# Four modulation sixths summed on TensorE from raw weight tiles, token-major gate values, and raw tiles issued earlier, in a one-core decoder layer

## The chip, the cores and the metric

The kernel runs on one core of a Trainium2 chip. The metric is the device time of one launch in microseconds; the time before is the median of three runs.

## What is computed

One layer over 2048 tokens of width 1024, all in fp32. A conditioning vector gives six modulation vectors, `mod = silu(c) @ w_ada + b_ada` (1024 by 6144), in the order shift1, scale1, gate1, shift2, scale2, gate2. Then:

```
h    = rms_norm(x, g_mix) * (1 + scale1) + shift1
proj = h @ w_in                       # gMLP u | v (512 each), q, k, v
a    = u' * (tril(w_s) @ v' + b_s)    # u', v' = gelu(u), gelu(v); chunks of 128 tokens, 8 groups of 64
b    = sliding-window attention with sinks (8 q heads, 2 kv heads, window 128)
x    = x + gate1 * (concat(a, b) @ w_out)
h2   = rms_norm(x, g_ffn) * (1 + scale2) + shift2
x    = x + gate2 * (relu(h2 @ w_ff1)**2 @ w_ff2)
y    = rms_norm(x, g_final)
```

## The kernel before

Activations lie feature-major: tiles of 128 channels by 512 tokens (a slab; there are four). Each product is made in three matmuls (`mm3`, L326 to L328): operands are split into a high part on ScalarE (L69, L293) and a low part on VectorE (L70, L294), and high by high, high by low and low by high are summed in PSUM. The feed-forward layer works on a pair of slabs with a Strassen-like scheme of seven products: `ffn_c` makes the first half and writes its forms to DRAM (`ad`), `ffn_d` reads them back in 56 steps, each of two tiles `w2w` and `aw` (128x1024) that are split into `w2h`, `w2l`, `ah`, `al` and feed 24 matmuls of 512 columns.

The stages follow each other in the order of the code: slab 0's input projections, slabs 1 and 2 with attention 0 and 1 woven in (145 to 505 us), `ffn_c(0)` (505 to 820 us), `ffn_d(0)` with `beside` (slab 3, attention 2 and 3, output projections 2 and 3) woven into it (820 to 1452 us), `ffn_c(1)` (1452 to 1760 us) and `ffn_d(1)` to the end. The side work is written as generators that are advanced between matmul groups (`step`, `weave`). A scheduler then fixes the order of each engine's queue; every queue is executed in order. Nearly all transfers are issued on SP's queue: `get` issues a load, `put` appends a store that is issued one or two loads later.

Tiles come from pools with fixed numbers of slots, and a new tile waits until a slot is free: `wk` has 12 (weights, raw tiles, halves), `xl` has 4 (x tiles, w2 quarters), the PSUM bank `ov` has one.

`ada_rest(ci)` (L187 to L206) makes one sixth of the modulation in two halves. A half loads four `adar` tiles (128x2x512), and VectorE sums the eight raw tiles times a scalar into `acc` (L196, the first on ScalarE, L198); then four matmuls against a column of ones sum over the partitions. An fp32 matmul stands in the trace as two instructions, so these are 8. `in_vu` makes the gate: values are computed feature-major, transposed on TensorE (`turn`, L532), split and multiplied by the spatial weights (`gate`, L546 to L548). `out_proj` loads the residual tile `xt` after the group that it is added to (L719). `final_norm` stores `y` at L1059.

Of the kernel before, what the change touches and what calls it, by code (L numbers as in the profile page):

```python
# [11 lines left out]
F32 = mybir.dt.float32  # L12
F32R = mybir.dt.float32r
# [4 lines left out]
P = 128  # L18
D = 1024
KT = D // P  # L20
# [29 lines left out]
def hybrid_block(ctx, tc, x_l, c_l, pos, wada0, wada, vec, win, wsT, bs, sinks, wout, w1, w2, rope_c, y_l):  # L50
# [135 lines left out]

    def ada_rest(ci):  # L187
        for half in range(2):
            acc = t2("acc")
            for k in range(KT):  # L190
                if k % 2 == 0:
                    two = wk("adar", F32, [P, 2, T])
                    get(two, wada[ci - 2, half, k:k + 2].rearrange("k p t -> p k t"))
                raw, sc = two[:, k % 2], cact[:, k:k + 1]
                if k:
                    dve.scalar_tensor_tensor(out=acc, in0=raw, scalar=sc, in1=acc, op0=ALU.mult, op1=ALU.add)  # L196
                else:
                    act.activation(out=acc, in_=raw, func=AF.Copy, scale=sc)  # L198
                if k % 4 == 3:
                    yield  # L200
            mp = ps.tile([P, 4], F32, name="modp", tag="ov", bufs=1)
            for j in range(4):
                pe.matmul(out=mp[:, j:j + 1], lhsT=acc[:, j * P:(j + 1) * P], rhs=ones[:, 0:1], start=True, stop=True)
            o = ci * KT + 4 * half
            dve.tensor_tensor(out=mod[:, o:o + 4], in0=mp, in1=vecs[:, o:o + 4], op=ALU.add)
            yield  # L206
# [307 lines left out]
    def in_vu(s, h, st, u0=None):  # L514
        vts, us = {}, {}
        sgu = list(wsp)
        if s > 0:
            ts = [m2("wsp", F32R, [P, 4, P]) for _ in range(4)]
            for t, d in zip(ts, wspd):
                get(t.bitcast(F32).rearrange("p g c -> p (g c)"), d, d)  # L520
            sgu = [ts[0:2], ts[2:4]]

        def gelu(bank, name):
            t = t2(name)
            act.activation(out=t, in_=bank, func=AF.Gelu_apprx_tanh)
            return t

        def turn(p):
            vf = vts.pop(p)
            vp = ps.tile([P, NB, P], F32, name="vq", tag="pt", bufs=2)  # L530
            for b in range(NB):
                pe.transpose(out=vp[:, b], in_=vf[:, b * P:(b + 1) * P], identity=ident)  # L532
            vh, vl = m2("vt", F32R, [P, NB, P]), m2("vt", F32R, [P, NB, P])
            act.activation(out=vh, in_=vp, func=AF.Copy)
            dve.tensor_tensor(out=vl, in0=vp, in1=vh, op=ALU.subtract)
            vts[p] = vh, vl

        def gate(p):
            u, (vh, vl) = us.pop(p), vts.pop(p)
            sv = t2("sv")  # L540
            w_h, w_l = (t[:, 2 * (p % 2):2 * (p % 2) + 2] for t in sgu[p // 2])
            for half in range(2):
                so = ps.tile([P, 2, 2, P], F32, name="so", tag="sc", bufs=2)
                for i in range(2):
                    b = 2 * half + i
                    pe.matmul(out=so[:, i], lhsT=vh[:, b], rhs=w_h, start=True, stop=False)  # L546
                    pe.matmul(out=so[:, i], lhsT=vl[:, b], rhs=w_h, start=False, stop=False)
                    pe.matmul(out=so[:, i], lhsT=vh[:, b], rhs=w_l, start=False, stop=True)  # L548
                for hh in range(2):
                    r0, r1 = hh * HD, (hh + 1) * HD  # L550
                    dve.tensor_tensor(out=sv[r0:r1, half * 2 * P:(half + 1) * 2 * P].rearrange("p (c t) -> p c t", c=2),
                                      in0=so[r0:r1, :, hh, :],
                                      in1=bsb[r0:r1, p, :].unsqueeze(1).broadcast_to([HD, 2, P]), op=ALU.add)
            dve.tensor_tensor(out=sv, in0=sv, in1=u, op=ALU.mult)
            put(mixd[s][p], mixd[s][p], sv)

        todo = []

        def behind():
            while todo:  # L560
                f, p = todo.pop(0)
                f(p)

        for pp in range(2):
            two = w_take(("i", 4 * pp), ("i", 4 * pp + 1)), w_take(("i", 4 * pp + 1), ("i", 4 * pp + 2 + (pp == 0 and u0 is not None)))
            for p in (2 * pp, 2 * pp + 1):
                o = bank()
                for k in range(KT):
                    c = (k % 4) * 2 * P + (p % 2) * P
                    mm3(o, *two[k // 4].cut(c, c + P), h[k], k == 0, k == KT - 1)  # L570
                vts[p] = gelu(o, "vf")
                behind()
                todo.append((turn, p))
                yield
            for p in (2 * pp, 2 * pp + 1):
                if p == 0 and u0 is not None:
                    us[p] = u0
                else:
                    us[p] = gelu(group(h, ("i", 4 * pp + 2 + p % 2), ("i", min(4 * pp + 3 + p % 2, 7))), "u")
                    behind()  # L580
                    yield
                todo.append((gate, p))
        behind()
        yield


# [127 lines left out]

    def out_proj(s, mix):
        stat = Stat()
        for d in range(KT):
            o = group(mix, ("o", d), ("o", min(d + 1, KT - 1)))
            xt = x_tile(s, d)  # L719
            x2 = t2("x2")  # L720
            dve.scalar_tensor_tensor(out=x2, in0=o, scalar=mod[:, 2 * KT + d:2 * KT + d + 1], in1=xt,  # L721
                                     op0=ALU.mult, op1=ALU.add)
            stat.add(x2)
            put(x2d[s][d], x2d[s][d], x2)
            yield
# [121 lines left out]
    def ffn_c(p, forms):  # L847
# [42 lines left out]
        for j in range(16):  # L890
# [20 lines left out]
            if j > 0:  # L911
                product(j, 2, x, False)
                b11 = relu2(p1, x)
            prep(j + 1, 1)
            yield
            q = bank("mm")
            product(j, 7, q, True)
# [12 lines left out]
            dve.tensor_tensor(out=u, in0=q, in1=u, op=ALU.add)  # L930
            b21 = relu2(u)
            prep(j + 1, 3)
            load(j + 2)
            for i, f in token_forms(b11, b12, b21, b22).items():
                if i not in (1, 3):
                    nc.sync.dma_start(out=ad[p, i, c][:, e], in_=f)
# [6 lines left out]
    def ffn_d(p, last):  # L943
# [29 lines left out]
            dve.tensor_tensor(out=dst, in0=src, in1=dst, op=ALU.add)  # L973

        order = (1, 6, 5, 3, 7, 4, 2)
        halves = {}

        def prep(n):
            if n >= 56 or n in halves:
                return  # L980
            i, c = order[n // 8], n % 8
            wraw, araw = wk("w2w", F32), wk("aw", F32, [P, 2, T])
# [6 lines left out]
            get(araw, ad[p, i, c])  # L989
            halves[n] = (halve(wraw, wk("w2h"), wk("w2l")),  # L990
                         halve(araw, wk("ah", F32R, [P, 2, T]), wk("al", F32R, [P, 2, T])))

        for m, i in enumerate(order):
            if i in (1, 3, 7, 4):
# [43 lines left out]
            if i == 7:  # L1038
                norm = final_norm(2 * p + 1, xs, 1, stats[1])
            if i == 2:  # L1040
                last.append(final_norm(2 * p, xs, 0, stats[0]))
            yield

    def final_norm(s, xs, t, stat):
        stat.finish("sc")
        yield
        stat.diag()
        yield
        rbc = stat.cast(t2("rbc"), "sc")
        yield  # L1050
        for d in range(KT):
            x = xs[d // 4, t, d % 4]
            if x is None:
                x = sb.tile([P, T], F32, name="xt", tag="xl", bufs=NXL)
                get(x, x3d[d // 4, t, d % 4], x3d[d // 4, t, d % 4])
            y = t2("y")
            dve.scalar_tensor_tensor(out=y, in0=x, scalar=gfin[:, d:d + 1], in1=rbc,
                                     op0=ALU.mult, op1=ALU.mult)
            nc.sync.dma_start(out=y_l[s, d], in_=y)  # L1059
            if d % 2:  # L1060
                yield

# [182 lines left out]
    def beside():  # L1245
        rb3, h3, m2_, m3_ = [], [], [], []
        st2, st3 = sts[2], sts[3]
        rope_load(3)
        yield from zipped(chain(qkv_back(2, st2), then_halo(2, late(attention, 2, st2)), late(qkv_back, 3, st3)),
                          chain(x_stats(3, rb3), h_build(3, rb3, h3), in_qkv(3, h3, st3), in_vu(3, h3, st3)))  # L1250
        yield from zipped(attention(3, st3), chain(blank(28), mix_build(2, m2_), out_proj(2, m2_)))
        yield from mix_build(3, m3_)
        yield from until(h2, "even")
        yield from out_proj(3, m3_)

    def blank(n):
        for _ in range(n):
# [82 lines left out]
```

## Time and profile before

| | us |
|---|---|
| median of three runs | 2080.46 (2079.78 to 2086.93) |
| profiled execution, its time | 2078.88 |
| profiled execution, span | 2077.1 |
| TensorE busy | 1921.9 |
| VectorE busy | 1419.1 |
| ScalarE busy | 911.2 |

The span runs from the first instruction to the last. TensorE's matmuls are pipelined, so its busy time isn't its time at its peak; the start-to-start distance of neighbouring matmuls is the measure used below. The granted clock is 1.00 at TensorE's upper level and 0.50 at the lower; over the span it is 0.968.

### The profile page before, as it was taken

The page shows a single profiled execution, that of the slowest core. Times are in us where ns is not written, and L with a number is a line of the kernel's source. Part 1 is how long each engine was busy: PE and PEld are TensorE (multiplying, and loading weights), DVE is VectorE, ACT ScalarE, POOL GpSimd, SP SyncE. Part 2 cuts the span into 40 slices and gives each one's busy share as a digit, 9 for nine tenths or more (in the row PEclk, how much of TensorE's full clock was granted, in tenths as well). Part 3 has the DMA queues.
Part 4 walks back from the last instruction along what each step waited for, and adds up shares of the span by engine and source line. Part 5 has one row for each costly group of instructions (what it writes and reads, how often), then busy time and mean ns, then how long its engine had stood idle before and what let it go on. Part 6 is the DMA issues. An engine that isn't in the chain of part 4 may idle for free.

```text
span 2077.1 us, 25303 instructions
## 1 busy us (share of the span) xinstructions
PE 1921.9 (93%) x8532; PEld 1565.3 (75%) x8532; DVE 1419.1 (68%) x2400; ACT 911.2 (44%) x1563; POOL 173.9 (8%) x234
## 2 busy tenths in 40 slices
PE   5998898888999899889978998988999999999997
PEld 4787676777877688768866786866888888888875
DVE  8677789659677766783577855596766665545675
ACT  3535554244444444543344534354444444434442
POOL 4402213100000000010011210000000000000000
PEclk9999898999999999999988999999999999999998
DMA  9995497892577857787666789684544446555663
GB/s 319 352 348 200 130 329 260 307 388 84 197 269 247 276 177 267 262 310 249 205 203 227 283 295 343 223 293 143 183 149 156 157 152 210 193 200 210 235 218 128
DMA packets 236210, 486.72 MB, mean 234 GB/s; under 512 B 23808, under 2 KB 81280, under 8 KB 236080
## 3 DMA queue, kind: packets, MB, share of 16 engines
q1 hardware_dynamic: 234960, 484.38, 67.1%
q8 instruction: 67, 1.10, 0.2%
q0 software_dynamic: 1120, 0.72, 0.1%
q14 instruction: 63, 0.52, 0.1%
HBM read 349.55 MB, written 135.46 MB: 233 GB/s over the span
## 4 chain that ended last, share of the span: by engine, by line
PE 48%; DMA 8%; DVE 5%; ACT 2%; issue 1%; SPq 1%; POOL 0%; POOLq 0%; DVEq 0%; ACTq 0%
PE mm L327 16%; PE mm L328 15%; PE mm L326 15%; DMA w2w<-in_w_dram 2%; DMA aw<-ad 1%; DVE al L70 1%; DMA w2w<-w2d 1%; DMA a<-in_w_dram 1%; DVE w2l L70 1%; DMA w2d<-a 1%; ACT w2h L69 1%; PE sc L625 1%; DMA xt<-x2d 1%; DMA s<-w2d 1%; SPq L93 1%
## 5 line engine op out<-in xcount | busy, mean ns | idle before, releaser
L327 PE MATMUL mm<-al,w2h 128*128 128x512 f32 x896 | 357.4, 399 | 10.0 <-DVE al L70 9.7
L328 PE MATMUL mm<-ah,w2l 128*128 128x512 f32 x896 | 354.2, 396 | 0.0
L326 PE MATMUL mm<-ah,w2h 128*128 128x512 f32 x896 | 316.7, 400 | 13.7 <-ACT ah L69 13.1
L70 DVE TENSOR_TENSOR w2l<-w2w,w2h 128x1024 fp32r<-128x1024 f32 x112 | 137.3, 1226 | 181.7 <-ACT w2h L69 173.0
L69 ACT ACTIVATE w2h<-w2w 128x1024 fp32r<-128x1024 f32 x112 | 118.6, 1059 | 296.6 <-DMA w2w<-w2d 156.3
L327 PEld LDWEIGHTS mm<-al,w2h 128*128 128x128 f32 x896 | 171.6, 192 | 55.4 <-DVE al L70 20.5
L326 PEld LDWEIGHTS mm<-ah,w2h 128*128 128x128 f32 x896 | 171.0, 192 | 53.4 <-ACT ah L69 17.7
L326 PE MATMUL mm<-h,whi 128*128 128x512 f32 x448 | 181.3, 414 | 22.8 <-ACT h L264 12.8
L328 PEld LDWEIGHTS mm<-ah,w2l 128*128 128x128 f32 x896 | 171.3, 191 | 34.9
L327 PE MATMUL mm<-h,whi 128*128 128x512 f32 x448 | 180.6, 404 | 2.9 <-DVE h L265 2.7
L328 PE MATMUL mm<-h,wlo 128*128 128x512 f32 x448 | 179.8, 402 | 1.0 <-DVE wlo L294 0.9
L70 DVE TENSOR_TENSOR al<-aw,ah 128x1024 fp32r<-128x1024 f32 x112 | 137.3, 1226 | 34.6 <-ACT ah L69 21.0
L69 ACT ACTIVATE ah<-aw 128x1024 fp32r<-128x1024 f32 x112 | 118.4, 1058 | 60.0 <-DVE w2l L70 21.9
L234 POOL TENSOR_TENSOR rs<-ms,mhalf 128x4 f32<-128x4 f32 x12 | 16.6, 1386 | 1313.9 <-DVE ms L232 1313.8
L326 PEld LDWEIGHTS mm<-h,whi 128*128 128x128 f32 x448 | 87.9, 197 | 43.9 <-ACT h L264 14.4
L326 PE MATMUL mm<-mix,whi 128*128 128x512 f32 x256 | 100.9, 399 | 15.4 <-DVE x L721 9.5
L326 PE MATMUL mm<-hw,wah 128*128 128x512 f32 x256 | 100.8, 394 | 10.5 <-ACT p L895 9.3
L327 PEld LDWEIGHTS mm<-h,whi 128*128 128x128 f32 x448 | 87.2, 195 | 22.4 <-DVE h L265 5.1
L328 PE MATMUL mm<-mix,wlo 128*128 128x512 f32 x256 | 100.9, 394 | 1.4 <-DMA wlo<-ko2l 0.5
L328 PEld LDWEIGHTS mm<-h,wlo 128*128 128x128 f32 x448 | 87.1, 194 | 19.4 <-DVE wlo L294 1.3
L326 PE MATMUL mm<-hw,wdh 128*128 128x512 f32 x256 | 100.0, 391 | 1.1 <-DVE w L918 1.1
L326 PE MATMUL mm<-hw,wbh 128*128 128x512 f32 x256 | 100.2, 391 | 0.6 <-DVE w L908 0.6
(253 smaller groups left out, 4051.3 us busy)
## 6 DMA issues: line engine op xcount, KB each, us to landing
aw<-ad SPq DMA_DIRECT2D x112, 512.0 KB, 5.1
r<-in_w_dram SPq DMA_DIRECT2D x64, 512.0 KB, 5.0
w2w<-w2d SPq DMA_DIRECT2D x64, 512.0 KB, 3.7
a<-in_w_dram SPq DMA_DIRECT2D x96, 256.0 KB, 4.0
ad<-wt SPq DMA_DIRECT2D x96, 256.0 KB, 2.2
w2w<-in_w_dram SPq DMA_DIRECT2D x96, 256.0 KB, 3.9
xt<-in_x_dram SPq DMA_DIRECT2D x80, 256.0 KB, 6.1
adar<-in_wada_dram SPq DMA_DIRECT2D x32, 512.0 KB, 6.1
```

Of the source, the lines that this page charges most:

```text
L69: act.activation(out=hi, in_=t, func=AF.Copy)
L70: dve.tensor_tensor(out=lo, in0=t, in1=hi, op=ALU.subtract)
L93: ins = nc.sync.dma_start(out=out, in_=in_)
L234: self.pow = pool.tensor_tensor(out=rs[:, :nb], in0=ms[:, :nb], in1=mhalf[:, :nb], op=ALU.pow)
L326: pe.matmul(out=out, lhsT=wh, rhs=h[0], start=first, stop=False, **kw)
L327: pe.matmul(out=out, lhsT=wh, rhs=h[1], start=False, stop=False, **kw)
L328: last_mm[0] = pe.matmul(out=out, lhsT=wl, rhs=h[0], start=False, stop=last, **kw)
L625: pe.matmul(out=sc[:, i, o:o + (P if b == 0 else 2 * P)], lhsT=qst[:, j], rhs=key, start=hl == 0, stop=hl == 1)
```

## The change

- `ada_rest`: the eight raw tiles are no longer summed on VectorE and ScalarE. All four `adar` tiles of a half stay in their `wk` slots until 32 fp32 matmuls (four column blocks by eight tiles, the raw tile as the weights, one column of `cact` as the moving operand) sum them in PSUM.
- `in_vu`: values are computed token-major: the activation is the stationary operand, 256 columns of the weight the moving one. The transposes are gone. The next weight is no longer taken a group ahead for the u groups.
- `out_proj`: the residual tile is loaded one step ahead.
- `ffn_c`: the raw tiles of step j+2 are loaded after the fourth of seven products in place of the last.
- `ffn_d`: `load` is split from `prep`, and the raw tiles of the step after are loaded as soon as a step's are split.
- `final_norm`: `y` is stored through `put`, but for the last slab pair's first half.
- `beside`: `out_proj(3)` is interleaved with the first half of `h2_build(1)`, which stood ahead of it.

```
 def ada_rest(ci):
     for half in range(2):
-        acc = t2("acc")
-        for k in range(KT):
-            if k % 2 == 0:
-                two = wk("adar", F32, [P, 2, T])
-                get(two, wada[ci - 2, half, k:k + 2]...)
-            raw, sc = two[:, k % 2], cact[:, k:k + 1]
-            if k:
-                dve.scalar_tensor_tensor(out=acc, in0=raw, scalar=sc, in1=acc, op0=ALU.mult, op1=ALU.add)
-            else:
-                act.activation(out=acc, in_=raw, func=AF.Copy, scale=sc)
-            if k % 4 == 3:
+        twos = []
+        for k in range(0, KT, 2):
+            two = wk("adar", F32, [P, 2, T])
+            get(two, wada[ci - 2, half, k:k + 2]...)
+            twos.append(two)
+            if k % 4 == 2:
                 yield
         mp = ps.tile([P, 4], F32, name="modp", tag="ov", bufs=1)
         for j in range(4):
-            pe.matmul(out=mp[:, j:j + 1], lhsT=acc[:, j * P:(j + 1) * P], rhs=ones[:, 0:1], ...)
+            for k in range(KT):
+                pe.matmul(out=mp[:, j:j + 1], lhsT=twos[k // 2][:, k % 2, j * P:(j + 1) * P],
+                          rhs=cact[:, k:k + 1], start=k == 0, stop=k == KT - 1)
...
 # in_vu
-    def turn(p): ...                  # 4 transposes, then vh, vl from PSUM
+    def tokens(pp):
+        w = w_take(("i", 4 * pp), ("i", 4 * pp + 1)), w_take(("i", 4 * pp + 1))
+        for half in range(2):
+            o = bank()
+            ov = o.rearrange("p (b c) -> p b c", b=2)
+            for b in range(2):
+                cols = slice((2 * half + b) * P, (2 * half + b + 1) * P)
+                for k in range(KT):
+                    hi, lo = w[k // 4].cut((k % 4) * 2 * P, (k % 4 + 1) * 2 * P)
+                    pe.matmul(out=ov[:, b], lhsT=h[k][0][:, cols], rhs=hi, ...)
+                    pe.matmul(out=ov[:, b], lhsT=h[k][1][:, cols], rhs=hi, ...)
+                    last_mm[0] = pe.matmul(out=ov[:, b], lhsT=h[k][0][:, cols], rhs=lo, ...)
+            vf = gelu(o, "vf")
+            vh, vl = m2("vt"), m2("vt")   # split from vf
...
 # out_proj
+    xts = [x_tile(s, 0)]
     for d in range(KT):
+        if d + 1 < KT:
+            xts.append(x_tile(s, d + 1))
         o = group(mix, ("o", d), ("o", min(d + 1, KT - 1)))
-        xt = x_tile(s, d)
+        xt = xts[d]
...
 # ffn_c
         prep(j + 1, 1)
+        load(j + 2)
         yield
...
         prep(j + 1, 3)
-        load(j + 2)
...
 # ffn_d
     def prep(n):
         if n >= 56 or n in halves:
             return
+        load(n)
+        wraw, araw = raws[n]
         halves[n] = (halve(wraw, wk("w2h"), wk("w2l")),
                      halve(araw, wk("ah", F32R, [P, 2, T]), wk("al", F32R, [P, 2, T])))
+        load(n + 1)
...
 # final_norm
-            nc.sync.dma_start(out=y_l[s, d], in_=y)
+            if late:
+                put(y_l, y_l[s, d], y)
+            else:
+                nc.sync.dma_start(out=y_l[s, d], in_=y)
...
 # beside
-        yield from until(h2, "even")
-        yield from out_proj(3, m3_)
+        yield from zipped(out_proj(3, m3_), until(h2, "even"))
```

## Rows read from the trace of the kernel before

**Rows 1.** The page's head: the span, then busy time by engine.

```profile
span 2077.1 us, 25303 instructions
...
PE 1921.9 (93%) x8532; PEld 1565.3 (75%) x8532; DVE 1419.1 (68%) x2400; ACT 911.2 (44%) x1563; POOL 173.9 (8%) x234
```

**Rows 2.** Stages: length, busy time and instructions by engine, granted clock, DMA share, GB/s.

```profile
145.00:400.00 255.00, 220.80 (x1039) 177.51 (x1038) 210.00 (x537) 123.00 (x330) 58.47 (x79) 0.94 0.70 242
...
505.00:820.00 315.00, 302.05 (x1306) 246.26 (x1307) 219.87 (x311) 138.52 (x200) 0.00 (x0) 0.98 0.67 229
820.00:1250.00 430.00, 396.66 (x1772) 320.51 (x1771) 289.61 (x598) 190.43 (x408) 55.51 (x65) 0.95 0.74 254
...
1350.00:1452.00 102.00, 88.97 (x355) 68.10 (x354) 78.71 (x106) 48.79 (x65) 0.00 (x0) 0.95 0.67 222
1452.00:1960.00 508.00, 508.00 (x2247) 420.73 (x2246) 311.18 (x381) 229.63 (x293) 2.45 (x1) 1.00 0.53 183
```

**Rows 3.** TensorE in order of time, 170 us: start, length, line, operation.

```profile
170.34 0.95 PE L203 MATMUL modp<-ones,acc 128*128 128x1 f32 x8
171.15 0.49 PE L327 MATMUL mm<-h,whi 128*128 128x512 f32 x1
```

**Rows 4.** The tile adar: instructions, nanoseconds least, median, most.

```profile
L196 DVE SCALAR_TENSOR_TENSOR acc<-adar,cact,acc x56: 711/744/754, 143.9 to 681.0; 128x512 f32<-128x512 f32 x56
...
L198 ACT ACTIVATE acc<-adar,cact x8: 707/722/724, 141.7 to 640.4; 128x512 f32<-128x512 f32 x8
```

**Rows 5.** TensorE in order of time, 28 us.

```profile
28.36 1.70 PE L178 MATMUL modp<-ones,acc 128*128 128x1 f32 x8
29.92 0.77 PE L328 MATMUL mm<-h,wlo 128*128 128x512 f32 x1
```

**Rows 6.** TensorE in order of time, 52 to 58 us.

```profile
52.45 1.05 PE L178 MATMUL modp<-ones,acc 128*128 128x1 f32 x8 [0.63 <-DVE mod L182]
54.28 3.36 PE L326 MATMUL mm<-h,whi 128*128 128x512 f32 x7 [0.77 <-ACT h L264]
```

**Rows 7.** Half microseconds there, columns as in rows 2.

```profile
53.50:54.00 0.50, 0.01 (x1) 0.00 (x0) 0.50 (x1) 0.50 (x1) 0.41 (x2) 1.00 1.05 426
...
54.50:55.00 0.50, 0.50 (x2) 0.41 (x3) 0.50 (x1) 0.50 (x1) 0.42 (x2) 0.50 1.00 410
```

**Rows 8.** TensorE, 221 us: first and last of twelve matmuls of 256 columns.

```profile
221.29 0.28 PE L546 MATMUL so<-wsp,vt 128*128 128x256 f32 x1
...
222.61 0.28 PE L548 MATMUL so<-wsp,vt 128*128 128x256 f32 x1
```

**Rows 9.** TensorE, 94 us: four transposes and the matmul behind them.

```profile
94.74 0.60 PE L532 MATMUL vq<-ident,vf 128*128 128x128 f32 x4
95.09 0.48 PE L326 MATMUL mm<-h,whi 128*128 128x512 f32 x1
```

**Rows 10.** What TensorE waited for, 820 to 1250 us: total, times, longest.

```profile
PE sc L625 <- DVE pr L628: 4.6, 3, 3.5
PE tpp L658 <- DVE pr L649: 4.4, 3, 2.2
```

**Rows 11.** What ScalarE waited for, 820 to 1250 us.

```profile
ACT w2h L69 <- DMA w2w<-w2d: 68.6, 18, 9.5
```

**Rows 12.** What TensorE waited for, 1250 to 1452 us.

```profile
PE mm L326 <- ACT ah L69: 10.3, 6, 3.4
PE mm L326 <- DVE x L721: 9.5, 1, 9.5
```

**Rows 13.** The chain that ended last: start, length, what.

```profile
1402.21 3.69 DMA w2w<-in_w_dram
...
1408.94 4.30 DMA w2w<-in_w_dram
```

**Rows 14.** What SP's queue waited for, 1960 us to the end.

```profile
SPq L1059 <- DVE y L1057: 28.4, 13, 23.2
```

**Rows 15.** What TensorE waited for, 505 to 820 us.

```profile
PE mm L326 <- ACT p L895: 9.3, 5, 3.9
```

More of the change, by code (lines that the diff above doesn't have):

```diff
@@ L188, in ada_rest @@
         for half in range(2):
-            acc = t2("acc")
-            for k in range(KT):
-                if k % 2 == 0:
-                    two = wk("adar", F32, [P, 2, T])
-                    get(two, wada[ci - 2, half, k:k + 2].rearrange("k p t -> p k t"))
-                raw, sc = two[:, k % 2], cact[:, k:k + 1]
-                if k:
-                    dve.scalar_tensor_tensor(out=acc, in0=raw, scalar=sc, in1=acc, op0=ALU.mult, op1=ALU.add)
-                else:
-                    act.activation(out=acc, in_=raw, func=AF.Copy, scale=sc)
-                if k % 4 == 3:
+            twos = []
+            for k in range(0, KT, 2):
+                two = wk("adar", F32, [P, 2, T])
+                get(two, wada[ci - 2, half, k:k + 2].rearrange("k p t -> p k t"))
+                twos.append(two)
+                if k % 4 == 2:
                     yield
@@ L202, in ada_rest @@
             for j in range(4):
-                pe.matmul(out=mp[:, j:j + 1], lhsT=acc[:, j * P:(j + 1) * P], rhs=ones[:, 0:1], start=True, stop=True)
+                for k in range(KT):
+                    pe.matmul(out=mp[:, j:j + 1], lhsT=twos[k // 2][:, k % 2, j * P:(j + 1) * P],
+                              rhs=cact[:, k:k + 1], start=k == 0, stop=k == KT - 1)
             o = ci * KT + 4 * half
@@ L526, in gelu @@
             return t
[L528 to L536, printed above, removed]
+        def tokens(pp):
[7 more added lines that the diff above has]
+                        hi, lo = w[k // 4].cut((k % 4) * 2 * P, (k % 4 + 1) * 2 * P)
+                        pe.matmul(out=ov[:, b], lhsT=h[k][0][:, cols], rhs=hi, start=k == 0, stop=False)
+                        pe.matmul(out=ov[:, b], lhsT=h[k][1][:, cols], rhs=hi, start=False, stop=False)
+                        last_mm[0] = pe.matmul(out=ov[:, b], lhsT=h[k][0][:, cols], rhs=lo, start=False,
+                                               stop=k == KT - 1)
+                vf = gelu(o, "vf")
+                vh, vl = m2("vt"), m2("vt")
+                act.activation(out=vh, in_=vf, func=AF.Copy)
+                dve.tensor_tensor(out=vl, in0=vf, in1=vh, op=ALU.subtract)
+                vts[pp, half] = tuple(t.rearrange("p (b c) -> p b c", b=2) for t in (vh, vl))
+                yield
@@ L538, in gate @@
         def gate(p):
-            u, (vh, vl) = us.pop(p), vts.pop(p)
+            u = us.pop(p)
             sv = t2("sv")
+            cols = slice((p % 2) * P, (p % 2 + 1) * P)
             w_h, w_l = (t[:, 2 * (p % 2):2 * (p % 2) + 2] for t in sgu[p // 2])
             for half in range(2):
+                vh, vl = vts[p // 2, half]
                 so = ps.tile([P, 2, 2, P], F32, name="so", tag="sc", bufs=2)
                 for i in range(2):
[L545 to L548, printed above, removed]
+                    pe.matmul(out=so[:, i], lhsT=vh[:, i, cols], rhs=w_h, start=True, stop=False)
+                    pe.matmul(out=so[:, i], lhsT=vl[:, i, cols], rhs=w_h, start=False, stop=False)
+                    pe.matmul(out=so[:, i], lhsT=vh[:, i, cols], rhs=w_l, start=False, stop=True)
@@ L555, in gate @@
             put(mixd[s][p], mixd[s][p], sv)
[L557 to L562, printed above, removed]
-        for pp in range(2):
[L565 to L573, printed above, removed]
+        for pp in range(2):
+            for _ in tokens(pp):
+                if pp and 1 in us:
+                    gate(1)
                 yield
             for p in (2 * pp, 2 * pp + 1):
[L576 to L580, printed above, removed]
+                us[p] = u0 if p == 0 and u0 is not None else gelu(group(h, ("i", 4 * (p // 2) + 2 + p % 2)), "u")
+                if p % 2:
+                    gate(p - 1)
+                if p > 0 or u0 is None:
                     yield
-                todo.append((gate, p))
-        behind()
+        gate(3)
         yield
@@ L975, in ffn_d, with load @@
         order = (1, 6, 5, 3, 7, 4, 2)
-        halves = {}
-        def prep(n):
-            if n >= 56 or n in halves:
+        raws, halves = {}, {}
+        def load(n):
+            if n >= 56 or n in raws:
                 return
             i, c = order[n // 8], n % 8
-            wraw, araw = wk("w2w", F32), wk("aw", F32, [P, 2, T])
+            wraw, araw = raws[n] = wk("w2w", F32), wk("aw", F32, [P, 2, T])
             if i in W2SRC:
@@ L989, in prep @@
             get(araw, ad[p, i, c])
+        def prep(n):
+            if n >= 56 or n in halves:
+                return
+            load(n)
+            wraw, araw = raws[n]
             halves[n] = (halve(wraw, wk("w2h"), wk("w2l")),
                          halve(araw, wk("ah", F32R, [P, 2, T]), wk("al", F32R, [P, 2, T])))
+            load(n + 1)
         for m, i in enumerate(order):
@@ L1040, in ffn_d, with final_norm @@
             if i == 2:
-                last.append(final_norm(2 * p, xs, 0, stats[0]))
+                last.append(final_norm(2 * p, xs, 0, stats[0], p == 0))
             yield
-    def final_norm(s, xs, t, stat):
+    def final_norm(s, xs, t, stat, late=True):
         stat.finish("sc")
```

## The prediction

> **What bounds the kernel now.** I read the page's head first: TensorE is busy 1921.9 of 2077.1 us and VectorE, the next, 1419.1 [rows 1]. So time on TensorE's queue costs the kernel directly, unless it falls into a hole. The view of stages shows where the holes are [rows 2]. In 1452 to 1960 us TensorE never pauses: 2247 matmuls in 508 us, one per 0.226 us at a granted clock of 1.00. That is the rate at which a stream of 512 columns runs, and nothing can be won there. Elsewhere two things are lost, idle time and time at the lower clock, which I count as one minus the granted clock times the stage. From 145 to 400 us that is 34.2 us idle and some 15 us of clock, together about 50 of 255; from 820 to 1250 us it is 33.3 and 21.5, about 55 of 430; from 1350 to 1452 us 13 and 5; from 505 to 820 us 13 and 6. The waits of TensorE in these stages say what the holes are made of. From 820 to 1250 us they are mostly attention steps held by VectorE (4.6 us before the scores, 4.4 before the transposes) [rows 10], while ScalarE, whose queue those steps share, stands 68.6 us before `w2h` until a `w2w` load lands [rows 11].
>
> **The modulation sums: TensorE's new work.** Before, a half of a sixth costs TensorE 8 instructions. They take from 170.34 to 171.15 us, when the next matmul starts: 0.81 us, 0.101 each [rows 3]. Afterwards it is 32 matmuls of two instructions, 64. What a one-column instruction costs doesn't depend on which column it is, since what it waits for is its own weight load; so a train takes 64 x 0.101 = 6.5 us, 5.66 more than before, and the eight halves 45.3 us.
>
> The trace has no train of 64. Two short ones show what happens to the clock. At 28 us, at the lower level, 8 take 29.92 - 28.36 = 1.56 us, 0.195 each [rows 5]. At 52 us TensorE idles 0.63 us, runs a train of 8, and idles 0.77 us; when matmuls begin at 54.28 us the granted clock, 1.00 at 53.5, is 0.50 [rows 6, 7], and 7 matmuls take 3.36 us where 1.58 would do, so 1.8 us are lost. [...] I therefore expect a train of 6.5 us to lose the clock about halfway: 32 x (0.195 - 0.101) = 3.0 us for its second half, and some 1.7 us for the matmuls behind it. Eight times 4.7 is 37.6 us. The bounds are no fall (0) and the lower level for a whole train and 1.8 us behind it, 64 x 0.094 + 1.8 = 7.8, eight times 62.
>
> The Trainium skill (TensorE: Matmul & The Clock Gate, Part 1) says that the gate follows how busy the array has recently been, and that the throttled state is the default, released by activity. Whether one column per weight load is activity, that part doesn't say. If it is, the trains cost 45.3 us; if it isn't, some 83 us.
>
> **What hides it.** VectorE loses 56 sums of 744 ns, 41.7 us, and ScalarE 8 of 722 ns, 5.8 us [rows 4]. Six of the eight halves lie between 145 and 400 us, where VectorE is busy 210 of 255 us and TensorE loses about 50. A train ahead of a wait shortens that wait, and 31 us less on VectorE shorten others. I let this take back 28 us, somewhat over half of the stage's loss; the bounds are 0 and 50. The last two halves stand in `ffn_c(0)`, where VectorE has room and nothing is hidden. Modulation in all: 45.3 + 37.6 - 28 = +55 us.
>
> **Token-major values.** Per slab 96 matmuls of 512 columns become 192 of 256. Twelve of these run from 221.29 to 222.61 us, 11 distances of 0.120 [rows 8]; 192 x 0.120 - 96 x 0.226 = +1.3 us, +5.4 for four slabs. Gone are 16 groups of four transposes, each 0.35 us to the next matmul, which is 0.09 us longer than the usual 0.39: 0.44 x 16 = -7.0 us [rows 9]. Splits and gelus keep their count. Sum -2 us. The u weights are no longer taken a group ahead. SP can issue them early all the same while `wk` has slots; only slab 0 also has to split them, and a split of some 2.3 us exposed at three groups would be +7, the upper bound.
>
> **The residual tile ahead, and `out_proj(3)` beside `h2`.** TensorE stands 9.5 us before an output projection whose residual add had no x tile [rows 12], and the clock falls behind it, which by the price above is 1.7 us. Both edits aim at this place: -11 us, between 0 and that.
>
> **Raw tiles earlier.** In `ffn_d` a load moves ahead by one step, so ScalarE should find its tile and let the attention steps behind it through. Of the 55 us lost from 820 to 1250 us I take two fifths, -22; the bounds are 0 and -55. From 1350 to 1452 us I take nothing. The loads of neighbouring steps come 6.7 us apart there [rows 13], not the 24 x 0.226 = 5.4 us of their matmuls: the `x3` tiles hold two of the twelve `wk` slots, two sets of halves hold eight, and so the raw tiles of the next step need the two slots that those of this step leave when they are split. Issuing them sooner doesn't free a slot. In `ffn_c` ScalarE's late tiles cost TensorE 9.3 us through `p1` [rows 15]. The earlier load helps these, but the four `adar` tiles now stay in `wk` until their matmuls, two steps later, in the same stage: I net it at -1 us, between -9 and +10.
>
> **The late store of y.** At the end SP stands 28.4 us before stores of `y` with weight loads behind them [rows 14]. Stored through `put`, they no longer hold the loads: -3 us (0 to -6, as TensorE idles little there).
>
> **Sum.** 55 - 2 - 11 - 22 - 1 - 3 = +16 us. The profiled execution took 2078.9 us, so 2094.9; it lies 1.6 us below the median of the runs shown, within their spread. I forecast 2095 us.
>
> **Rivals.** *The trains are nearly free.* If the array counts them as work, or other matmuls are ordered between their instructions, the clock holds and the 37.6 us vanish. Then 45.3 - 28 - 39 = -22 us: 2057. For it speaks VectorE's 82% in the stage of six halves; against it the fall behind a short train [rows 6, 7]. It ends on the faster side and decides from the point where a train costs less than about 8.5 us, since then the sum crosses zero.
>
> *The slots run out.* In `ffn_d` raw tiles held a step longer bring one step's use to ten of twelve `wk` slots, and each side weight with its successor wants four. Then the side weights come late in place of the raw tiles; the 22 us are not won, and a late weight behind perhaps a dozen side groups at 1 us each adds 12: 2095 + 34 = 2129. That this limit binds already, with two slots less, is in [rows 13]; against it, a stretch of `beside` uses few weights.
>
> *The edits do little.* TensorE's holes take the trains, and the loads move while their waits go elsewhere: 2079 give or take 10.
>
> **How the numbers follow.** About 10 us, 0.5%, is what a measurement of this kernel can tell from no change. The forecast has 0.42 and runs from 2080 to 2115 (0.12 of it within 0.5%, 0.30 above). The free trains have 0.30, from 2035 to 2072 (0.28 below, 0.02 within). The slots have 0.18, 2115 to 2145, all above. The last has 0.10 (0.06 within, 0.04 below). Faster 0.32, same 0.20, slower 0.48. The range that leaves out 2 in 10, the far ends of both outer cases, is 2045 to 2132; the forecast's own is 2080 to 2115.
>
> **What the changed profile would show.** The trains: `modp` at L199 or so with 512 instructions, 0.10 us apart, with a granted clock of 0.50 in their second half and behind them; at 0.10 throughout and 1.00 behind them the first rival holds. VectorE's busy time lower by about 42 us. No `vq`. From 145 to 400 us TensorE's idle time well under 34 us, though the stage is longer. From 820 to 1250 us ScalarE's 68.6 us before `w2h` at less than half; if they stay, or TensorE waits for `whi` and `wlo` loads, the slots are the cause. The 9.5 us wait gone. From 1350 to 1452 us the step stays near 7 us. The forecast is wrong if the trains don't stand as blocks in TensorE's queue, or if the attention steps wait for something other than ScalarE's late tiles.

## The result and the profile after

The changed kernel takes 2130.3 us (median of 4 runs), the kernel before 2080.1 beside it: a ratio of 1.0235 (95% interval 1.0206 to 1.0263), by which it is some 49 us slower. The forecast was 2095 and its own stretch 2080 to 2115; the time lies above that, and just inside the upper end of the whole range, 2132. The profiled execution took 2132.8 us, its span is 54.0 us longer than before. Line numbers of the changed kernel stand a few lines off: `mm3` is L323 to L325, `out_proj`'s residual add L717, `y`'s store L1065.

The page's head of after [rows 1]. TensorE works 79.5 us longer, VectorE 32.8 us less:

```profile
span 2131.1 us, 26776 instructions
...
PE 2001.4 (94%) x9300; PEld 1662.7 (78%) x9300; DVE 1386.3 (65%) x2344; ACT 912.7 (43%) x1559; POOL 170.4 (8%) x234
```

To see where the time went, cut the span at the first scores matmul, the first one of `ffn_c(0)`, of `ffn_d(0)` and of `ffn_c(1)`; these starts are read from the rows of the tiles `qst`, `wah` and `w2h`. Lengths in us, of profiled executions (between kernels with the same code in a stage they differ by up to 6):

| | slab 0 | attention stage | `ffn_c(0)` | woven `ffn_d(0)` | rest, to the last norm |
|---|---|---|---|---|---|
| before | 151.1 | 340.7 | 331.8 | 620.3 | 619.8 |
| after | 160.7 | 353.9 | 362.1 | 621.8 | 619.2 |
| only the modulation | 154.3 | 358.6 | 353.2 | 617.2 | 620.0 |
| all but the modulation | 158.8 | 339.3 | 333.4 | 620.8 | 619.2 |
| only token-major | 157.3 | 335.6 | 334.8 | 624.7 | 620.0 |

The loss is 9.6 + 13.2 + 30.3 us in the first three stages. The woven stage, where the forecast had 22 + 11 us to gain, is as long as it was, within what profiled executions differ by.

One train in after, TensorE in order of time, at the end of slab 0, and the windows around it (columns as in rows 2):

```profile
150.86 8.97 PE L199 MATMUL modp<-cact,adar 128*128 128x1 f32 x64
159.68 0.77 PE L323 MATMUL mm<-h,whi 128*128 128x512 f32 x1
...
161.96 0.63 PE L323 MATMUL mm<-h,whi 128*128 128x512 f32 x1
162.39 0.63 PE L324 MATMUL mm<-h,whi 128*128 128x512 f32 x1
```

```profile
150.80:154.20 3.40, 3.40 (x32) 3.36 (x31) 3.35 (x9) 3.35 (x15) 0.00 (x0) 1.00 0.91 309
154.20:159.60 5.40, 5.40 (x35) 5.40 (x34) 4.78 (x13) 1.50 (x3) 0.00 (x0) 0.67 1.03 394
159.60:166.50 6.90, 6.90 (x23) 5.80 (x23) 3.17 (x16) 1.21 (x7) 0.00 (x0) 0.52 0.83 300
```

Here is the mechanism of the forecast: a block of 64; its first half at 1.00 and 0.106 us each; its second half at a falling clock, 5.4 us; then matmuls at 0.52. Until 166.23 us, where the distances are the usual ones again, these are 11 of 512 columns, most of them 0.43 us apart where 0.227 is usual, and eight of 128 columns: 3.2 us lost, not 1.7. All eight trains, by the starts of their first instruction and of what follows, without idle time, last 8.5 to 13.5 us, 82.2 in sum (6.4 before); behind each of them, against the usual distances, 1.5 to 3.2 us are lost, 19 in sum. One stands in slab 0, five in the attention stage, two in `ffn_c(0)`. Three of them are cut by a few other matmuls. The last had the lower clock from its start: TensorE had stood 4.2 and 2.0 us before it, and the train took 13.5 us.

```profile
730.79 0.79 PE L323 MATMUL mm<-hw,wbh 128*128 128x512 f32 x1 [4.21 <-ACT wbh L69]
```

```profile
738.40:751.90 13.50, 13.50 (x65) 13.49 (x64) 6.23 (x9) 1.69 (x2) 0.00 (x0) 0.50 0.80 272
```

The three stages in after, by windows. The same view of before over its own stages, 151 to 492, 492 to 824 and 824 to 1452 us, has TensorE idle for 39.5, 17.8 and 56.1 us at a clock of 0.94, 0.98 and 0.95:

```profile
150.80:514.70 363.90, 356.19 (x1946) 314.76 (x1946) 245.05 (x590) 161.37 (x397) 59.13 (x81) 0.91 0.71 251
514.70:877.00 362.30, 342.45 (x1481) 283.55 (x1480) 229.78 (x329) 148.27 (x216) 0.00 (x0) 0.93 0.60 205
877.00:1505.00 628.00, 574.60 (x2581) 460.91 (x2580) 420.77 (x779) 274.48 (x520) 56.04 (x70) 0.95 0.74 254
```

In the attention stage 7.7 us of idle time are left: the trains stand in the holes. In `ffn_c(0)` there were few to fill. The third row is that of before within 3 us in busy time, and equal in clock.

What TensorE waits for in the woven stage (total, times, longest, us), in before from 824 to 1452 us and in after from 877 to 1505, and below it ScalarE there, in the same order:

```profile
PE mm L326 <- ACT ah L69: 13.1, 10, 3.4
...
PE mm L327 <- DVE al L70: 6.5, 10, 1.3
```

```profile
PE mm L323 <- ACT ah L69: 17.8, 15, 5.1
PE mm L324 <- DVE al L70: 11.3, 13, 2.5
PE tpp L651 <- DVE pr L642: 5.4, 3, 2.6
PE sc L618 <- DVE pr L621: 3.3, 3, 1.7
...
PE mm L323 <- DVE x L717: 1.2, 2, 0.8
```

```profile
ACT w2h L69 <- DMA w2w<-w2d: 74.9, 20, 9.5
ACT w2h L69 <- DMA w2w<-in_w_dram: 50.0, 15, 5.6
...
ACT w2h L69 <- PE mm L327: 9.6, 3, 3.8
```

```profile
ACT w2h L69 <- DMA w2w<-w2d: 55.9, 15, 8.6
ACT w2h L69 <- DMA w2w<-in_w_dram: 45.1, 14, 7.5
ACT w2h L69 <- PE mm L324: 41.8, 8, 8.8
```

The 9.5 us before a residual add [rows 12] are gone. But the waits before `ah` and `al`, 13.1 + 6.5 = 19.6 us in before, are 29.1 here: 9.5 more. The attention steps that VectorE holds (`sc` and `tpp` before `pr`) wait 8.7 us, 9.0 before [rows 10]. And ScalarE still waits for loads 101.0 us, 124.9 before, and 41.8 for matmuls that free the slots of the halves, 9.6 before.

### The profile page after: what moved, and what is told of

The parts are those of the page before. It is cut to its first block, busy times and chain, and to the rows that moved or that the text cites. A ratio compares the mean times of both kernels' runs of the same rounds, so it can differ in the third digit from the quotient of the medians.

```text
span 2131.1 us, 26776 instructions
## 1 busy us (share of the span) xinstructions
PE 2001.4 (94%) x9300; PEld 1662.7 (78%) x9300; DVE 1386.3 (65%) x2344; ACT 912.7 (43%) x1559; POOL 170.4 (8%) x234
## 4 chain that ended last, share of the span: by engine, by line
PE 64%; DMA 16%; DVE 10%; ACT 4%; issue 3%; SPq 2%; POOL 2%; DVEq 0%; POOLq 0%; ACTq 0%
PE mm L324 18%; PE mm L325 18%; PE mm L323 18%; PE modp L199 3%; DMA w2d<-a 3%; DMA a<-in_w_dram 2%; DMA w2w<-w2d 2%; DMA w2w<-in_w_dram 1%; SPq L93 1%; PE mm L534 1%; PE mm L535 1%; PE mm L536 1%; DMA aw<-ad 1%; DMA s<-w2d 1%; DVE al L70 1%
## 5 line engine op out<-in xcount | busy, mean ns | idle before, releaser
L325 PE MATMUL mm<-ah,w2l 128*128 128x512 f32 x896 | 355.1, 397 | 0.0
L323 PE MATMUL mm<-ah,w2h 128*128 128x512 f32 x896 | 314.5, 401 | 19.5 <-ACT ah L69 17.8
L323 PEld LDWEIGHTS mm<-ah,w2h 128*128 128x128 f32 x896 | 170.4, 193 | 60.9 <-ACT ah L69 24.3
L325 PEld LDWEIGHTS mm<-ah,w2l 128*128 128x128 f32 x896 | 172.1, 192 | 35.1
L69 ACT ACTIVATE ah<-aw 128x1024 fp32r<-128x1024 f32 x112 | 118.4, 1057 | 60.9 <-DMA aw<-ad 31.4
L323 PE MATMUL mm<-h,whi 128*128 128x512 f32 x320 | 128.2, 412 | 12.1 <-ACT h L261 10.0
L324 PE MATMUL mm<-h,whi 128*128 128x512 f32 x320 | 130.5, 408 | 3.8 <-DVE h L262 3.8
L325 PE MATMUL mm<-h,wlo 128*128 128x512 f32 x320 | 128.9, 403 | 1.7 <-DVE wlo L291 1.6
L323 PE MATMUL mm<-hw,wbh 128*128 128x512 f32 x256 | 101.0, 395 | 4.7 <-ACT wbh L69 4.7
L323 PE MATMUL mm<-mix,whi 128*128 128x512 f32 x256 | 101.4, 399 | 3.4 <-ACT mix L702 2.0
L325 PE MATMUL mm<-hw,wbl 128*128 128x512 f32 x256 | 100.9, 394 | 2.6 <-DVE wbl L70 2.6
L325 PE MATMUL mm<-hw,wal 128*128 128x512 f32 x256 | 101.0, 395 | 1.9 <-DVE wal L70 1.9
L325 PE MATMUL mm<-hw,wdl 128*128 128x512 f32 x256 | 100.5, 393 | 1.8 <-DVE wdl L70 1.8
L325 PE MATMUL mm<-mix,wlo 128*128 128x512 f32 x256 | 101.7, 397 | 0.5 <-DVE wlo L291 0.2
L324 PE MATMUL mm<-mix,whi 128*128 128x512 f32 x256 | 101.3, 397 | 0.0
```

What stands on the lines that cost most here:

```text
L69: act.activation(out=hi, in_=t, func=AF.Copy)
L323: pe.matmul(out=out, lhsT=wh, rhs=h[0], start=first, stop=False, **kw)
L324: pe.matmul(out=out, lhsT=wh, rhs=h[1], start=False, stop=False, **kw)
L325: last_mm[0] = pe.matmul(out=out, lhsT=wl, rhs=h[0], start=False, stop=last, **kw)
```

## The experiments

Ratios are to the kernel before, run beside each on the same chip (2078 to 2080 us).

| run | median, us | ratio (95%) |
|---|---|---|
| a_only | 2116.4 | 1.0163 (1.0134 to 1.0192) |
| no_a | 2089.8 | 1.0042 (1.0030 to 1.0054) |
| raw_only | 2083.2 | 1.0010 (0.9996 to 1.0024) |
| b_only | 2088.0 | 1.0037 (1.0018 to 1.0057) |
| cgf | 2081.5 | 1.0018 (1.0001 to 1.0036) |
| a_spread | 2121.4 | 1.0174 (1.0138 to 1.0211) |
| after_oldload | 2124.9 | 1.0234 (1.0198 to 1.0270) |
| after_hold | 2123.3 | 1.0226 (1.0192 to 1.0260) |
| raw_xl5 | 2072.3 | 0.9966 (0.9946 to 0.9986) |
| before_xl5 | 2078.5 | 1.0006 (0.9992 to 1.0020) |
| raw_wk13 | 2076.6 | 0.9986 (0.9969 to 1.0002) |
| midprep | 2078.3 | 1.0005 (0.9988 to 1.0022) |
| nolate | 2050.8 | 0.9855 (0.9831 to 0.9879) |
| nolate_raw | 2050.3 | 0.9850 (0.9821 to 0.9879) |
| nolate_raw_wk13 | 2052.4 | 0.9870 (0.9847 to 0.9893) |
| late_early | 2066.6 | 0.9948 (0.9933 to 0.9963) |
| late_early_cg | 2069.6 | 0.9948 (0.9927 to 0.9969) |

**The two halves of the change.** `a_only` is before with the new `ada_rest`, `no_a` is after with the old one.

> Only the modulation on TensorE, all else as before. Theory 1 (the modulation carries the whole loss, the other edits are worth nothing): 2130 us, +50, with about 23 us of it before the feed-forward part and about 25 in the first feed-forward half. Theory 2 (the modulation costs about the +55 forecast or more and the other edits win some back): 2150 or more. Theory 3 (the other edits lose too): 2105 or less.

> The whole change without the modulation on TensorE. Theory 1: within 10 us of before. Theory 2: 2045 to 2065. Theory 3: 2095 or more. The trace should show the 9.5 us wait before the output projection gone, and in the woven ffn_d ScalarE waiting for TensorE to free slots where it waited for w2w loads before.

The modulation alone costs 1.63%, 34 us; all the rest, of which the forecast hoped for 39 us, costs 0.42%, 9 us. That lies between theories 1 and 3: the modulation isn't the whole loss, and the other edits lose a little. In `a_only` the attention stage has TensorE idle for 9.7 of 358.6 us, 39.5 before, and its clock is 0.90; `ffn_c(0)` is 21.4 us longer:

```profile
154.30:512.90 358.60, 348.87 (x1713) 298.93 (x1711) 233.65 (x565) 151.77 (x376) 57.39 (x81) 0.90 0.69 242
512.90:866.00 353.10, 336.03 (x1486) 278.65 (x1485) 230.84 (x330) 147.22 (x215) 0.00 (x0) 0.95 0.62 211
```

**The parts of the rest.** `b_only` has token-major values alone; `cgf` the residual tile ahead, `out_proj(3)` interleaved, the late store of `y` and `ffn_c`'s earlier load; `raw_only` the split of `load` from `prep` in `ffn_d`:

```
-        def prep(n): ...                # loads, then splits
+        def load(n): ...                # raws[n] = w2w, aw
+        def prep(n):
+            load(n); wraw, araw = raws[n]; ...
+            load(n + 1)
```

> Only the token-major values. Forecast's step: 2079, -2, with no transposes. Rival (weights of the u groups no longer taken a group ahead, so that slab 0's splits stand in the way): 2084 to 2092, the first attention scores about 7 us later than before.

> Only the small edits: residual tile a step ahead, out_proj(3) beside h2, the late store of y, the earlier raw load in ffn_c. Forecast's steps: -11 -3 -1, 2066. Rival (the woven stage is paced by its loads through the slots, so that a wait taken from one place comes back in another): within 8 us of before though the 9.5 us wait is gone.

> Only the split of load and prep in ffn_d, the raw tiles a step earlier. Forecast's step (late loads hold up ScalarE and the attention steps behind it): 2058, -22. Rival (the twelve slots bind): within 10 us of before, ScalarE's waits for w2w loads replaced by waits for TensorE at w2h. Second rival (side weights come later): up to +20.

Token-major is slower by 0.37%, 8 us, as its rival said. Its stream runs as forecast [rows 8]; between these two matmuls lie 14 distances, 0.120 us each:

```profile
92.82 0.28 PE L537 MATMUL mm<-whi,h 128*128 128x256 f32 x1
...
94.50 0.28 PE L539 MATMUL mm<-wlo,h 128*128 128x256 f32 x1
```

What it loses is in slab 0, where TensorE idles 7.3 us from 60 to 165 us, 1.9 before. The longest wait there begins with a load. SP issues it at 72.10 us in before and, since it is no longer taken a group ahead, at 79.67 in `b_only`; ScalarE stands before its split, and the copy `qf`, for which TensorE waits, stands behind that split in ScalarE's queue:

```profile
72.10 0.70 SPq L93 DMA_DIRECT2D raw<-in_win_dram  x1
```

```profile
79.67 2.93 SPq L93 DMA_DIRECT2D raw<-in_win_dram  x3
...
85.68 1.06 ACT L293 ACTIVATE whi<-raw 128x1024 fp32r<-128x1024 f32 x1 [5.94 <-DMA raw<-in_win_dram]
...
87.27 0.39 PE L537 MATMUL mm<-whi,h 128*128 128x256 f32 x1 [3.76 <-ACT qf L430]
```

`cgf` gains nothing (0.18% slower; its interval barely leaves out 1), nor does `raw_only` (0.10%), in which ScalarE's waits for loads are not replaced by waits for slots either: 109.9 and 18.7 us, 124.9 and 9.6 before. In `cgf` the 9.5 us before `x` are gone, and from 829 to 1452 us TensorE waits 33.5 us before `ah` and `al`:

```profile
PE mm L326 <- ACT ah L69: 22.2, 17, 3.2
PE mm L327 <- DVE al L70: 11.3, 12, 3.4
```

In `raw_only` the loads hardly come earlier. SP's issue of one `aw` and ScalarE's start of its split:

```profile
827.36 0.33 SPq L93 DMA_DIRECT2D aw<-ad  x1
```

```profile
833.45 1.06 ACT L69 ACTIVATE ah<-aw 128x1024 fp32r<-128x1024 f32 x1 [1.02 <-DMA aw<-ad]
```

That is 6.1 us. Over the 56 steps the median is 6.3 us, 6.4 in before, 6.9 in after; of these, 5.1 us pass until an `aw` has landed (median in before). In program order the load stands a step earlier, in time it doesn't.

**What holds the loads.** SP's queue is executed in order. `w2_late` is side work that makes the weight forms of products 3 and 7 (the late forms below) from quarters in `xl` tiles (`a`) and stores them (`w2d`). In before's woven stage SP stands 63.3 us until such stores land, which is when their `xl` slots come free, and 60.9 us until matmuls free a `wk` slot (69.1 and 38.3 in after):

```profile
SPq L93 <- DMA w2d<-a: 63.3, 26, 4.9
SPq L93 <- PE mm L328: 60.9, 27, 9.0
```

So these were tried: one slot more in either pool (`NWK` 13, `NXL` 5), with constants cut down to make room; the late forms left out, so that products 3 and 7 read raw quarters; and the split moved to the middle of a step with the load at its top:

```
# raw_wk13, raw_xl5 (and before_xl5, without raw_only's edit)
-NT, NM, NWK, NXL = 9, 60, 12, 4
+NT, NM, NWK, NXL = 9, 60, 13, 4     # or 12, 5; bsb and others shrunk
# nolate, nolate_raw
+    W2SRC = {1: (0, 0), 2: (2, 0), 4: (2, 2), 3: (0, 2), 7: (0, 0)}
-        if 2 <= n < 22:
-            step(s4 if n < 18 else s3)
...
# midprep, in a step's loop of groups
+                    prep(8 * m + c + 1)      # half the side steps before, half behind
+                    yield
```

> Raw tiles a step earlier with 13 wk slots in place of 12 (room made by leaving out most of the spatial bias, the first mask and one of two halos, so those parts are computed wrongly). If wk slots bind: ScalarE's 18.7 us of waits for TensorE at w2h nearly gone and 2055 to 2075. If SP's queue binds: 2078 to 2090.

> Raw tiles a step earlier with 5 xl slots in place of 4 (room made by leaving out most of the spatial bias). If SP standing before xl slots binds: SP's 67.7 us of waits for w2d stores clearly less and 2055 to 2075. If wk slots bind: 2078 to 2090.

> The kernel before with 5 xl slots (most of the spatial bias left out). If raw_xl5's 6 us came from the slot alone: 2070 to 2076. If it needs the earlier loads as well: 2077 to 2083.

> As raw_only, with the split of the next step's tiles moved behind half of a step's side work, while its load stays at the step's top. If ScalarE's waits for w2w loads (110 us in raw_only) are what makes the woven stage slow: these waits under 50 us and 2050 to 2070. If they cost nothing, as other work was not ready either: the waits fall and the time is within 10 us of before.

> The kernel before with the forms of w2 for products 3 and 7 left out of ffn_d (w2_late isn't run; those products read raw quarters, so part of the computation is changed). It takes away 48 of the loads and 32 of the stores that share SP's queue and the four xl slots with the side work. If SP's queue, held by xl slots, is what makes the woven stage slow: 2050 or less. If it is the wk slots or the attention steps themselves: within 12 us of before.

> The same with the raw tiles loaded a step earlier. If the earlier load failed only because SP stood before xl slots: at least 10 us below the kernel without it (nolate). If the twelve wk slots bind: within 6 us of it, with ScalarE's waits for TensorE at w2h present.

> As nolate_raw, with 13 wk slots in place of 12 (most of the spatial bias, a mask and a halo left out). If, once SP no longer stands before xl slots, the wk slots are the next limit: SP's 122 us of waits for TensorE well down and 2030 to 2043. If not: 2046 to 2055.

None of them wins the 22 us. With a `wk` slot more, `raw_only`'s edit stands at 0.9986, not to be told from no change; its time lies between the two expected stretches. With an `xl` slot more it stands at 0.9966, 7 us, and its interval leaves out 1. Its time, 2072.3 us, lies in the stretch expected if the `xl` slots bind, but the sign named with it fails: SP's waits for the `w2d` stores are 64.6 us, 67.7 in `raw_only`. The gain is under the 0.5% that count here, and the woven stage of its profile, 617.0 us, is only 3.3 below before's. Whether slot and load win a little together stays open; the slot alone wins nothing (`before_xl5`). The median from issue to split is 6.2 to 6.4 us in the five of these kernels with the edit. In `midprep`, ScalarE's waits for loads stayed too, 114.2 us from 824 to 1440 us.

Only leaving out the late forms moves the stage, from 620.3 to 590.1 us, much as expected (2050 or less), and then the earlier load is worth nothing either (591.8; 2050.8 and 2050.3 us). With them gone SP stands for `wk` slots instead, in `nolate_raw` from 825 to 1420 us:

```profile
SPq L93 <- PE mm L328: 122.1, 35, 7.8
```

and one slot more doesn't change that (2052.4). What of the late forms holds the stage isn't told apart by these runs: leaving them out takes 80 transfers from SP's queue and the DMA engines and also 32 subtractions of 0.69 us, 22 us, from VectorE. That a fifth `xl` slot wins nothing alone speaks against the slots.

**The modulation inside the whole.** `ffn_c(0)` takes 362.1 us in after, 353.2 in `a_only`. Three kernels are after with one thing changed each: `a_spread` cuts each train into four pieces of 16 instructions and advances the side work faster to fit them; `after_oldload` puts `ffn_c`'s load back; `after_hold` advances the modulation there in neighbouring steps, so that the `adar` tiles hold their slots for a shorter time.

```
# a_spread: ada_rest, behind each column block
+                if j < 3:
+                    yield
# after_oldload: ffn_c
-            load(j + 2)                 # after the fourth product
+            load(j + 2)                 # after the last
# after_hold: ffn_c(0)
-        if n > 13 and n % 9 == 1:
+        if n in (20, 21, 22, 48, 49, 50):
```

> The changed kernel with each train of 64 instructions cut into four of 16, other work of the same queue between them, and the side work stepped faster so that the halves come at about the same places. If the lower clock is a part of the trains' cost: 0.10 us per instruction throughout, granted clock back to about 0.97, and 2095 to 2105. If the cost is the 512 weight loads alone, or the places change nothing: 2120 to 2135.

> The changed kernel with ffn_c's raw load back at its old place behind the last product. If the earlier load and the adar tiles that stay in the slots collide: ffn_c(0) from 362 us to about 353 as with the modulation alone, and about 2120. If they don't: 2126 to 2134.

> The changed kernel with the three steps of a modulation half in ffn_c(0) close together, so that its four adar tiles hold slots for a third of the time. If held slots are a part of ffn_c(0)'s 30 us: that stage at 350 us or less and about 2118 to 2124. If the trains alone make it: 358 to 366 us and 2125 to 2135.

Pieces that stood alone ran at 0.106 us an instruction, and the matmuls behind them 0.23 us apart, the first 0.32:

```profile
616.64 1.84 PE L199 MATMUL modp<-cact,adar 128*128 128x1 f32 x16
618.34 0.49 PE L325 MATMUL mm<-hw,wch 128*128 128x512 f32 x1
```

`ffn_c(0)` is 18 us shorter than in after (344.1) and its clock 0.97, where it is 0.93 in after:

```profile
514.00:860.00 346.00, 325.38 (x1468) 267.55 (x1467) 229.46 (x330) 146.68 (x214) 0.00 (x0) 0.97 0.62 211
```

That is 12.3 us over before, and the two trains' 128 instructions at 0.106 us, less the 16 that they replace, are 12 (lengths of one stage differ by up to 6 us): with the clock near before's 0.98, there the clock's part of the price is gone, and the weight loads' part stays. In the attention stage most pieces came together again in blocks of 4.6 to 10 us, and that stage gained nothing (357.3). In sum 1.0174 against 1.0235. The time, 2121.4 us, lies in the stretch expected if the places change nothing; in `ffn_c(0)` the trace shows the other case.

The old place of the load gives a profiled `ffn_c(0)` of 351.3 us, but the ratio doesn't fall (1.0234). Shorter holding of the slots leaves the stage at 361.1. Neither time, 2124.9 and 2123.3 us, decides between what was expected. Part of the 9 us by which that stage is longer in after than in `a_only` is the train that had the lower clock from its start: 13.5 us, 9.8 in `a_only`. That the two halves of the change cost more together (2.35%) than apart (1.63% + 0.42%) is within the intervals and needs no cause.

**A faster version.** If the late forms hold the woven stage, they can be made in `ffn_c(0)`, where the DMA engines are less busy (in before a share of 0.65 from 492 to 824 us, 0.74 in the woven stage). `late_early` is before with most of their steps there; `late_early_cg` adds the residual tile ahead and the interleaved `out_proj(3)`.

```
+    s4, s3 = w2_late(3), w2_late(7)     # ahead of ffn_c(0)
...
+        if n > 28 and n % 5 == 2:
+            step(s4)
+        if n > 13 and n % 6 == 4:
+            step(s3)
...                                      # ffn_d(0)
-        if 2 <= n < 22:
-            step(s4 if n < 18 else s3)
-        elif n < 30:
-            step(s3)
+        if n < 8:
+            step(s4)
```

> The kernel before with the w2_late work moved from the woven ffn_d(0) into ffn_c(0), nothing left out. If the work is dear only beside the side work: the woven stage at about 592 us, ffn_c(0) a little over 332, 2055 to 2065. If it is paid for wherever it stands: within 10 us of before.

> late_early with the residual tile a step ahead and out_proj(3) beside h2. If the wait before the output projection (9.9 us in late_early) is worth its length once the w2_late work is gone from the stage: 2055 to 2059, the woven stage at about 590 us. If it comes back elsewhere even so: 2063 to 2071, that wait gone and the other waits of the stage longer by as much.

`late_early` beats both kernels: 2066.6 us, 0.52% faster than before (0.37% to 0.67%), a little short of the 2055 to 2065 expected. `ffn_c(0)` takes 8.1 us more, the woven stage 19.8 less. The two edits on top win nothing. The woven stage of `late_early` and TensorE's waits in it, and below those of `late_early_cg`:

```profile
831.50:1432.00 600.50, 555.69 (x2486) 450.72 (x2485) 403.03 (x747) 273.20 (x518) 54.03 (x70) 0.96 0.69 236
```

```profile
PE mm L326 <- ACT ah L69: 12.8, 13, 4.3
PE mm L326 <- DVE x L721: 9.9, 1, 9.9
...
PE mm L327 <- DVE al L70: 3.1, 5, 1.2
```

```profile
831.90:1433.20 601.30, 556.17 (x2474) 450.31 (x2473) 401.84 (x747) 272.49 (x518) 57.16 (x70) 0.96 0.68 235
```

```profile
PE mm L326 <- ACT ah L69: 18.2, 12, 3.0
PE mm L327 <- DVE al L70: 7.0, 8, 2.0
```

The wait of 9.9 us is gone, those before `ah` and `al` are 9.3 us longer, and TensorE idles 45.1 us in the stage, 44.8 without the two edits.

## Why the prediction was wrong

The side was right, the size was not: +16 us forecast, +49 measured. Taken apart by the runs, the terms are, with the ends of their 95% intervals:

| term | forecast | measured alone |
|---|---|---|
| modulation | +55 | +34 (`a_only`; 28 to 40) |
| token-major | -2 | +8 (`b_only`; 4 to 12) |
| residual tile, `out_proj(3)`, `ffn_c`'s load, `y` | -15 | +4 (`cgf`; 0 to 7) |
| raw tiles earlier in `ffn_d` | -22 | +2 (`raw_only`; -1 to 5) |

The four together make 48 us. The modulation was forecast 21 us too dear and the three others 53 us too cheap in sum, so that the forecast missed by no more than 33 us is in part luck.

**The step that failed most: "Raw tiles earlier", -22 us.** It read ScalarE's 68.6 us before `w2h` [rows 11] as loads that are issued too late by the program's order. They are issued when SP gets to them and a slot is free, and that is as late with the edit as without: 6.3 us from issue to split, 6.4 before. The prediction had said this itself of 1350 to 1452 us ("Issuing them sooner doesn't free a slot") and did not carry it to 820 to 1250. By its own sign (these waits at less than half, or the slots are the cause) the slots should be what holds the loads, as ScalarE's waits for `w2d` loads are 55.9 us in after; but a thirteenth slot (`raw_wk13`) doesn't win the 22 us, so that reading isn't shown either. The attention steps that the earlier tiles should have let through wait in after as long as before, 8.7 us and 9.0 [rows 10]; those 9.0 were little over a quarter of the 33.3 us that TensorE idled from 820 to 1250 us. The step distance at the stage's end is as forecast; the loads in the chain of waits of after [rows 13] come 6.9 and 6.2 us apart:

```profile
1465.84 3.89 DMA w2w<-in_w_dram
1472.77 3.20 DMA w2w<-in_w_dram
1479.00 3.29 DMA w2w<-in_w_dram
```

The second half of the error is that even loads that did come early won nothing: in `raw_only` four of the 56 steps had theirs 20 to 33 us ahead of the split, and the stage stayed; four steps are few to tell by. A wait of ScalarE, which is busy for 272 of 628 us there, isn't yet a wait of TensorE: in after its waits for loads are 24 us shorter and the stage isn't. That the late forms hold some 30 us of this stage is shown by `nolate`, and 20 of them went with moving the work, of which 8 came back in `ffn_c(0)`; by what path they hold it, and what makes up the rest of the stage's loss, stays open.

**"The residual tile ahead", -11.** The wait went as forecast, and its time came back before `ah` and `al` in after, in `cgf` and in `late_early_cg`. One wait taken out of this stage was not time won; what sets its pace isn't shown.

**Token-major, -2.** The rate of the stream was right. The bound named for slab 0, +7, has the right size, as slab 0 is 6.2 us longer in `b_only`, but not the right path. The prediction let SP issue the weights early all the same and feared the splits; SP issued one 7.6 us later, and ScalarE's 5.9 us before it, ahead of a copy that TensorE needed, are what was lost.

**The modulation, +55.** The price of a train was nearly right: 8 x 9.5 = 76 us forecast with its slow half, 82.2 measured (82.1 in `a_only`), and 8 x 1.7 = 14 us behind them, 19 measured (18 in `a_only`). The clock fell about halfway, as forecast, in four of the eight trains of after; in the other four it fell sooner or was at 0.50 from the start. So the first rival, in which the clock holds, fell. Gross, the trains cost 82.1 + 18.2 - 6.4 = 94 us in `a_only`. The Trainium skill (TensorE: Matmul & The Clock Gate, Part 1) says that the gate follows how busy the array has recently been; of the two sums that the prediction worked out beside it, 45.3 and some 83 us, the trace is nearer to the second. What was too small is the cover, 28 us: 94 - 34 = 60. Trains filled TensorE's holes in the attention stage almost wholly. By stages of `a_only`, six trains cost 21 us up to its end, where 6 x 10.4 - 28 = 34 were forecast; with 71 us gross that is a cover of 50. The two in `ffn_c(0)`, taken as uncovered, cost 21.4, where 20.7 were.

**The second rival**, slots that run out, is nearest in time (2129), but that is luck: the woven stage, where it would have lost 12 us to late side weights, is unchanged, and TensorE waits for no `whi` and 0.2 us for `wlo` there.

**The late store of y, -3.** The 28.4 us [rows 14] were misread. One wait of 23.2 us is most of them; it stands behind the last load and before stores that the change leaves as they were. In after:

```profile
2099.37 0.54 SPq L93 DMA_DIRECT2D aw<-ad  x1
2123.16 4.97 SPq L1065 DMA_DIRECT2D out_dram<-y  x8
```

SP waits 25.0 us there, so only 3.4 us stood before stores with loads behind them, and the rest of the kernel is 0.6 us shorter:

```profile
SPq L1065 <- DVE y L1060: 25.0, 8, 23.2
```

## What to carry to other kernels

Before a load is moved earlier in the code, look up what its queue waits for ahead of it: what sets the issue may be a slot or a store, and then the order of the code doesn't. Work on a bound engine costs nothing only in that engine's holes, so price it stage by stage. A wait removed from a stage full of other waits should be counted as nothing until a run shows otherwise. The largest gain here came from leaving one piece of side work out to see what it holds, and then moving it.

## What the runs showed of the hardware

A train of 64 one-column fp32 instructions at 150.86 us in after starts at the upper clock, 0.106 us each, and ends at the lower one, and the matmuls behind it run at 0.52 for 6.9 us more. Sixteen such instructions between dense matmuls kept the upper clock and that price, here from 616.60 to 618.30 us in `a_spread`:

```profile
616.60:618.30 1.70, 1.70 (x17) 1.66 (x16) 1.70 (x4) 0.00 (x0) 0.00 (x0) 1.00 0.80 267
618.30:620.30 2.00, 2.00 (x11) 1.64 (x11) 0.16 (x1) 0.00 (x0) 0.00 (x0) 1.00 1.03 401
```

The same 512 instructions take 82.2 us in blocks, and 72.2 where part of them are spread.
